# A 32-phase Toeplitz convolution with tree-added LayerNorm statistics, and engine orders from a list scheduler, in a two-layer convolutional decoder trunk

## The chip, the cores and the metric

The kernel runs on the eight NeuronCores of one Trainium2 chip, four on each of two dies. Each core takes one prompt sequence of 2048 positions and 16 decoding sequences of 4 positions, so T = 2112 columns per core, with all weights. The cores do not talk to one another. The time is the device time of the slowest core in microseconds. Some executions of these kernels fall into a slow state, in which the cores of one die show a lower TensorE clock.

TensorE does matrix products into PSUM (eight banks of 512 fp32 columns), VectorE and ScalarE elementwise work, GpSimd (POOL) small copies and the issue of weight loads, SyncE (SP) the issue of the other transfers.

## The reference, cut to what matters

```python
def hybrid_layer(x, ...):                            # twice, then a last RMSNorm
    h = rmsnorm(x, norm_g)
    p = h @ w_in                                     # (T, 7168): a_val, a_gate, z_a, B, C, hb, z_b
    u = a_val * sigmoid(a_gate)
    ca = causal_dwconv(u, width 31)                  # per channel, over positions
    ca = head_layernorm(ca + bias)                   # per token over the 128 channels of a head, 8 heads
    y_a = silu(ca) * silu(z_a)
    y_b = B * causal_dwconv(C * hb, width 3) * silu(z_b)
    return x + concat(y_a, y_b) @ w_out
```

It also returns the last 30 rows of u and the last 2 of C * hb of each sequence. For the decoding sequences 26 of the 30 rows are old ones, copied from input to output by two transfers from memory to memory, one for each layer.

## The kernel before

Activations lie with channels on partitions and columns along the free dimension, in four blocks of 512 and one of 64. A projection of one 128-channel chunk and one block is eight accumulating matmuls. The width-31 convolution is a Toeplitz product: u is written to memory and gathered back so that partitions hold 16 channels x 8 phases (position modulo 8). With 8 phases, 31 taps need five shifts:

```python
PH, CG, NG, NSH = 8, 16, 8, 5
...
for g in range(8):                                   # one head: 8 groups of 16 channels
    bk = pw.next()
    mm_group(bk, banks[bk][:, 0:UROW],               # UROW = 336 columns
             [(toep[:, half, (gg * NSH + s) * 128:...], up_sb[:, g, 64 - 16 * s:UPROW - 16 * s]) for s in range(NSH)], ...)
    P.op("dve", ... tensor_copy(co_sb[...], banks[bk][:, 0:UROW]) ...)
    if lj is not None:                               # LayerNorm statistics of the head before, between the groups
        if 2 <= g < 7: ln_var(g - 2)                 # matmul with 1/128, then Ln
        if g < 5: ln_center(l, lj, g)                # matmul with 0.5*(I - 1/128), then Square
```

Its result goes to memory and back into the channel layout, and the statistics are taken there, with two 512-column matmuls for each block. The Toeplitz blocks are built by VectorE as mask times weights. The order on every engine is the order in which the program writes its operations, interleaved by hand. Weights rotate through seven slots. The state copy of each layer stands late in its layer.

Of the kernel before, what the change touches and what calls it, by code (L numbers as in the profile page):

```python
# [12 lines left out]
D = 1024  # L13
# [14 lines left out]
PH = 8  # L28
CG = 16
NG = 8  # L30
NSH = 5
LANES = 16
UROW = 16 + 64 + 256
UPROW = 64 + UROW
NW = 7
VROW = 272
K_SAME = 3
# [4 lines left out]
class Res:  # L42
    __slots__ = ("name", "w", "r")

    def __init__(self, name):
        self.name = name
        self.w = None
        self.r = []


class Op:
    __slots__ = ("eng", "fn", "deps", "idx", "sig", "cnt", "chan", "name")


class Prog:
    ENGS = ("pe", "act", "dve", "pool", "sp")

    def __init__(self):
        self.ops = {e: [] for e in self.ENGS}
        self.chan_ops = {}  # L60

    def op(self, eng, fn, reads=(), writes=(), chan=None, name=""):
        o = Op()
        o.eng, o.fn, o.chan, o.name = eng, fn, chan, name
        o.sig = False
        o.cnt = 0
        o.idx = len(self.ops[eng])
        deps = set()
        for r in reads:
            if r.w is not None:  # L70
                deps.add(r.w)
        for w in writes:
            if w.w is not None:
                deps.add(w.w)
            for x in w.r:
                deps.add(x)
        deps.discard(o)
        keep = []
        for d in deps:
            if d.chan is None and chan is None and d.eng == eng:  # L80
                if eng == "pe":
                    continue
                if o.idx - d.idx > K_SAME:
                    continue
            keep.append(d)
            d.sig = True
        o.deps = keep
        for r in reads:
            r.r.append(o)
        for w in writes:  # L90
            w.w = o
            w.r = []
        self.ops[eng].append(o)
        if chan is not None:
            self.chan_ops.setdefault(chan, []).append(o)
        return o

    def emit(self, nc, block, sems, chan_sems, final_waits):
        for e in self.ENGS:
            c = 0  # L100
            for o in self.ops[e]:
                if o.chan is None and o.sig:
                    c += 1
                    o.cnt = c
        for ch, lst in self.chan_ops.items():
            c = 0
            for o in lst:
                c += 16
                o.cnt = c
        chan_total = {ch: 16 * len(lst) for ch, lst in self.chan_ops.items()}  # L110

        def run(eng_name):
            def body(e):
                waited = {}
                for o in self.ops[eng_name]:
                    need = {}
                    for d in o.deps:
                        s = chan_sems[d.chan] if d.chan is not None else sems[d.eng]
                        if need.get(s.num, (None, 0))[1] < d.cnt:
                            need[s.num] = (s, d.cnt)  # L120
                    for num, (s, c) in need.items():
                        if waited.get(num, 0) < c:
                            e.wait_ge(s, c)
                            waited[num] = c
                    ins = o.fn(e)
                    if o.chan is not None:
                        ins.then_inc(chan_sems[o.chan], 16)
                    elif o.sig:
                        ins.then_inc(sems[eng_name], 1)
                if eng_name == "sp":  # L130
                    for ch in final_waits:
                        if ch in chan_total:
                            e.wait_ge(chan_sems[ch], chan_total[ch])
            return body

        block.tensor(run("pe"))
        block.scalar(run("act"))
        block.vector(run("dve"))
        block.gpsimd(run("pool"))
        block.sync(run("sp"))  # L140


class Rot:
    def __init__(self, ids):
        self.ids = list(ids)
        self.i = 0

    def next(self):
        v = self.ids[self.i % len(self.ids)]
        self.i += 1  # L150
        return v


def build_nc(wseq=None):


    record = wseq is None
    wused = []
    nc = bass.Bass("TRN2", target_bir_lowering=False)
    P = Prog()  # L160
# [14 lines left out]
    wt_d = din("wt_d", [DEPTH, 8, 128, NG * NSH * PH])  # L175
    cw_b_d = din("cw_b", [128, DEPTH, 8, WB])
    vecs_d = din("vecs", [128, 72])
    hist_a_d = din("hist_a", [DEPTH, 8, 128, NG, 64])
    hist_b_d = din("hist_b", [128, DEPTH, 8, (WB - 1) * NS])
    sa_orig = din("sa_orig", [DEPTH, NS, WA - 1, D])  # L180
    cmat_d = din("cmat", [128, 2, 128])
# [7 lines left out]
    scr_c = dint("scr_c", [DEPTH, 8, 128, PH * UROW], BF16)  # L189
# [3 lines left out]

    x_sb = sb("x_sb", [128, KC * T], F32)
    h_sb = sb("h_sb", [128, KC * T], BF16)
    y_sb = sb("y_sb", [128, 6, T], BF16)
    u_sb = sb("u_sb", [128, 2, PH, UROW], BF16)
    up_sb = sb("up_sb", [128, NG, UPROW], BF16)
    toep = sb("toep", [128, 2, 4 * NSH * 128], BF16)
    co_sb = sb("co_sb", [128, 2, 4, UROW], BF16)  # L200
    cn_sb = sb("cn_sb", [128, PH, UROW], BF16)
    vbuf = sb("vbuf", [128, PH + 2, VROW], BF16)
    wsl = sb("wsl", [128, NW, 1024], BF16)
    wt_sb = sb("wt_sb", [128, 2, NG * NSH * PH], BF16)
    sq = sb("sq", [128, 2, 1024], BF16)
    th_t = sb("th_t", [128, 2, 512], F32)
    sz_t = sb("sz_t", [128, 2, 512], F32)
    rs_t = sb("rs_t", [128, T], F32)
    oat = sb("oat", [128, 3, NOA], F32)
    obt = sb("obt", [128, 8, NOB], F32)  # L210
    histb = sb("histb", [128, DEPTH, 8, (WB - 1) * NS], BF16)
    cmat = sb("cmat_sb", [128, 2, 128], F32)
    mask = sb("mask_sb", [128, 128], BF16)
    cb16 = sb("cb16", [128, 128], BF16)
    ones_s = sb("ones_s", [128, 128], BF16)
    ones_v = sb("ones_v", [128, 128], BF16)
    vecs = sb("vecs_sb", [128, 72], F32)
    cbias = sb("cbias", [128, 16], F32)
    cw_b = sb("cw_b_sb", [128, DEPTH, 8, WB], F32)
    banks = [es.enter_context(nc.psum_tensor(f"psb{i}", [128, 512], F32)) for i in range(8)]  # L220

    R = Res
    x_r = [[R(f"x{k}_{q}") for q in range(NB)] for k in range(KC)]
    h_r = [[R(f"h{k}_{q}") for q in range(NB)] for k in range(KC)]
    y_r = [[R(f"y{s}_{q}") for q in range(NB)] for s in range(6)]
    u_r = [[R(f"u{i}_{q}") for q in range(NB + 1)] for i in range(3)]
    up_r, uph_r = R("up"), R("uph")
    toep_r = [R("toep0"), R("toep1")]
    co_r = [[R(f"co{h}_{g}") for g in range(4)] for h in range(2)]
    cn_r = u_r[2]  # L230
    v_r = [R(f"v{q}") for q in range(NB)]
    vh_r = R("vh")
    w_r = [R(f"w{i}") for i in range(NW)]
    wt_r = [R("wt0"), R("wt1")]
    sq_r = [R("sq0"), R("sq1")]
    th_r = [R("th0"), R("th1")]
    sz_r = [R("sz0"), R("sz1")]
    rs_r = [R(f"rs{q}") for q in range(NB)]
    oat_r = [R("oat0"), R("oat1"), R("oat2")]
    obt_r = [R(f"obt{j}") for j in range(8)]  # L240
    vecs_r, cmat_r, cwb_r, histb_r = R("vecs"), R("cmat"), R("cwb"), R("histb")
    mask_r, cb16_r, ones_r, cbias_r = R("mask"), R("cb16"), R("ones"), R("cbias")
    bank_r = [R(f"bank{i}") for i in range(8)]
    scru_r = [[R(f"scru{l}_{j}") for j in range(8)] for l in range(DEPTH)]
    scrc_r = [[[R(f"scrc{l}_{j}_{h}") for h in range(2)] for j in range(8)] for l in range(DEPTH)]

    def u_view(i):
        return cn_sb if i == 2 else u_sb[:, i]

    pa, pw, pr = Rot([0, 1, 2, 3]), Rot([0, 1, 2]), Rot([4, 5, 6, 7])  # L250
    rot_th, rot_sz, rot_sq = Rot([0, 1]), Rot([0, 1]), Rot([0, 1])
# [9 lines left out]
    def blk(ap, q):  # L261
        if q < 4:
            return ap.rearrange("p (a c) -> p a c", a=2)
        return ap.rearrange("p (a c) -> p a c", a=4)

    def u_blk(ap, q):
        if q < 4:
            return ap[:, 2 * q:2 * q + 2, 80:UROW]
        return ap[:, 0:4, 0:16]

    def v_blk(q, lag):
        if q < 4:
            return vbuf[:, 2 * q + 2 - lag:2 * q + 4 - lag, 0:256]
        return vbuf[:, 2 - lag:6 - lag, 256:272]


    bg = []

    def pop(n=1):
        for _ in range(n):  # L280
            if bg:
                bg.pop(0)()


    wstate = {"loaded": 0, "next": 0}

    def w_prefetch(upto):
        if record:
            return
        while wstate["loaded"] < min(upto, len(wseq)):  # L290
            i = wstate["loaded"]
            s = i % NW
            kind, l, c = wseq[i]
            src = w_in_r[l, c] if kind == "in" else w_out_r[l, c]
            P.op("pool", (lambda e, s=s, src=src: e.dma_start(out=wsl[:, s, :], in_=src)),  # L295
                 reads=([x_r[7][0]] if i == 2 else []), writes=[w_r[s]], chan=f"w{s}", name=f"wload{i}")
            wstate["loaded"] += 1

    def w_get(*keys):
# [585 lines left out]
```

## Time and profile before

| | before |
|---|---|
| median of fast and slow runs, by session | 1334.5 to 1338.9 us |
| span of the profiled run | 1334.8 us |
| TensorE busy | 1215.7 us |
| VectorE, ScalarE, GpSimd busy | 715.7, 495.2, 135.4 us |
| TensorE work at issue cost (worked out in the prediction) | 1169 us |

The issue cost of a matmul is the time from its start to the next one's start in a dense run; the work is the sum of these. Three numbers make the time: this work, what TensorE's busy time has over it (matmuls at half clock, and drains: the end of the last matmul before a gap), and TensorE's idle time. The prediction works out all three and shows the lines. In a view, L318 is line 318 of that run's kernel.py; a line of waits ends with the total in us, how often, and the longest.

### The profile page before, as it was taken

What the parts mean: (1) busy time and instruction counts of PE and PEld (TensorE: products, weight loads), DVE (VectorE), ACT (ScalarE), POOL (GpSimd) and SP (SyncE); (2) the same over time, 40 slices, a digit from 0 to 9 for tenths busy, and PEclk for the clock granted to TensorE, in tenths of its full rate; (3) what the DMA queues carried; (4) which work ended last, traced back from release to release, by engine and by line L of the source; (5) the groups of instructions that cost most, each with busy time, mean ns of one, the idle gap of its engine ahead of it and who ended that gap; (6) DMA issues with size and microseconds to landing.
All of it is one profiled execution on the core that took longest, in us unless ns stands there. A gap on an engine that the chain in (4) does not pass through costs nothing.

```text
span 1334.8 us, 20305 instructions; the slowest of 8 cores (1324.8 to 1334.8 us)
## 1 busy us (share of the span) xinstructions
PE 1215.7 (91%) x6682; PEld 573.9 (43%) x6682; DVE 715.7 (54%) x1297; ACT 495.2 (37%) x805; POOL 135.4 (10%) x264
## 2 busy tenths in 40 slices
PE   3778999989998999999989699999999899999986
PEld 1233444444443444444444344444444344444442
DVE  4443445467564484445652345546746548444555
ACT  4430555551554402222331055555055440222232
POOL 1011111100101001000010211110010100100000
PEclk9898999999999999999989899999999999999988
DMA  9317655523436113212020674542343610322033
GB/s 266 67 52 136 161 128 128 108 41 73 100 64 124 24 17 59 37 32 37 1 42 18 153 176 116 117 116 64 62 102 54 136 25 16 56 41 32 13 130 131
DMA packets 88101, 108.61 MB, mean 81 GB/s; under 512 B 24960, under 2 KB 60288, under 8 KB 87552
## 3 DMA queue, kind: packets, MB, share of 16 engines
q0 software_dynamic: 39824, 41.30, 21.0%
q1 hardware_dynamic: 47744, 65.82, 15.6%
q8 instruction: 57, 0.93, 0.3%
q14 instruction: 44, 0.36, 0.1%
q10 hardware_dynamic: 432, 0.19, 0.1%
HBM read 116.85 MB, written 35.14 MB: 114 GB/s over the span
## 4 chain that ended last, share of the span: by engine, by line
PE 86%; DMA 5%; DVE 3%; issue 3%; ACT 2%; DVEq 0%; SPq 0%; POOL 0%; ACTq 0%; POOLq 0%
PE psb L318 85%; DMA wsl<-w_in_r 3%; PE psb L382 1%; DMA x_sb<-x_d 1%; DMA cn_sb<-scr_c 1%; ACT rs_t L530 1%; DVE x_sb L628 1%; ACT sq L368 0%; DVE h_sb L400 0%; DVE sz_t L614 0%; DVE toep L474 0%; ACT L392 0%; ACT rs_t L392 0%; DMA scr_c<-co_sb 0%; DVE co_sb L491 0%
## 5 line engine op out<-in xcount | busy, mean ns | idle before, releaser
L318 PE MATMUL psb<-h_sb,wsl 128*128 128x512 bf16 (+1 forms) x4480 | 819.9, 346 | 36.0 <-DMA wsl<-w_in_r 24.4
L318 PEld LDWEIGHTS psb<-h_sb,wsl 128*128 128x128 bf16 x4480 | 381.8, 99 | 474.7 <-issue 61.0
L628 DVE TENSOR_TENSOR x_sb<-x_sb,psb 128x512 f32<-128x512 f32 (+1 forms) x240 | 138.7, 592 | 62.9 <-PE psb L318 58.9
L318 PE MATMUL psb<-y_sb,wsl 128*128 128x512 bf16 (+1 forms) x800 | 160.1, 343 | 8.2 <-DVE x_sb L628 6.7
L318 PE MATMUL psb<-up_sb,toep 128*128 128x336 bf16 x640 | 110.9, 308 | 20.8 <-ACT rs_t L530 10.6
L579 DVE TENSOR_TENSOR vbuf<-psb,th_t 128x512 bf16<-128x512 f32 (+1 forms) x80 | 47.5, 597 | 134.5 <-PE psb L318 121.6
L605 DVE SCALAR_TENSOR_TENSOR rs_t<-vbuf,cw_b_sb,rs_t 128x512 f32<-128x512 bf16 (+1 forms) x160 | 104.9, 655 | 18.1 <-POOL vbuf L588 9.4
L430 DVE SCALAR_TENSOR_TENSOR u_sb<-th_t,psb 128x512 bf16<-128x512 f32 (+1 forms) x70 | 41.5, 593 | 132.7 <-PE psb L318 91.1
L575 ACT ACTIVATE th_t<-psb 128x512 f32<-128x512 f32 (+1 forms) x80 | 41.3, 516 | 183.3 <-PE psb L318 183.3
L318 PEld LDWEIGHTS psb<-y_sb,wsl 128*128 128x128 bf16 x800 | 69.1, 98 | 87.0 <-issue 14.0
L491 DVE CAST co_sb<-psb 128x336 bf16<-128x336 f32 x128 | 64.5, 507 | 71.8 <-PE psb L318 71.4
L427 ACT ACTIVATE th_t<-psb 128x512 f32<-128x512 f32 (+1 forms) x80 | 41.3, 517 | 142.8 <-PE psb L318 140.5
L610 ACT ACTIVATE sz_t<-psb 128x512 f32<-128x512 f32 (+1 forms) x80 | 41.8, 522 | 139.4 <-PE psb L318 139.4
L561 ACT ACTIVATE sz_t<-psb 128x512 f32<-128x512 f32 (+1 forms) x80 | 40.0, 521 | 133.2 <-PE psb L318 132.4
L368 ACT ACTIVATE sq<-x_sb 128x1024 bf16<-128x1024 f32 (+1 forms) x60 | 53.3, 903 | 97.2 <-DVE x_sb L628 77.8
L563 DVE TENSOR_TENSOR y_sb<-rs_t,sz_t 128x512 bf16<-128x512 f32 (+1 forms) x80 | 46.5, 598 | 79.7 <-ACT sz_t L561 79.7
L295 POOL DMA_DIRECT2D wsl<-w_in_r x112 | 60.2, 544 | 258.3 <-PE psb L318 241.3
L318 PEld LDWEIGHTS psb<-up_sb,toep 128*128 128x128 bf16 x640 | 57.5, 97 | 65.0 <-issue 38.8
L551 ACT ACTIVATE rs_t<-rs_t,vecs_sb 128x512 f32<-128x512 f32 (+1 forms) x80 | 57.5, 734 | 42.3 <-DVE rs_t L548 42.0
L318 PE MATMUL psb<-y_sb,toep 128*128 128x512 bf16 (+1 forms) x320 | 71.4, 348 | 0.0
L382 PE MATMUL psb<-sq,ones_s 128*128 128x512 bf16 (+1 forms) x120 | 34.0, 380 | 33.6 <-ACT sq L368 23.5
L548 DVE SCALAR_TENSOR_TENSOR rs_t<-psb,cbias,rs_t 128x512 f32<-128x512 f32 (+1 forms) x80 | 49.7, 651 | 27.0 <-ACT rs_t L507 27.0
(59 smaller groups left out, 749.6 us busy)
## 6 DMA issues: line engine op xcount, KB each, us to landing
wsl<-w_in_r POOLq DMA_DIRECT2D x112, 256.0 KB, 6.3
up_sb<-scr_u SPq DMA_DIRECT2D x16, 672.0 KB, 8.9
scr_c<-co_sb SPq DMA_DIRECT2D x32, 336.0 KB, 2.9
cn_sb<-scr_c SPq DMA_DIRECT2D x16, 672.0 KB, 7.9
scr_u<-u_sb SPq DMA_DIRECT2D x14, 672.0 KB, 3.7
x_sb<-x_d SPq DMA_DIRECT2D x3, 2048.0 KB, 19.4
wsl<-w_out_r POOLq DMA_DIRECT2D x24, 256.0 KB, 4.4
oa_copy<-sa_orig SPq DMA_DIRECT2D x2, 1664.0 KB, 15.1
```

Of the source, the lines that this page charges most:

```text
L295: P.op("pool", (lambda e, s=s, src=src: e.dma_start(out=wsl[:, s, :], in_=src)), reads=([x_r[7][0]] if i == 2 else []), writes=[w_r[s]], c ...
L318: ins = e.matmul(out, lhsT=l_, rhs=r_, start=(i == 0), stop=(i == len(pairs) - 1))
L368: P.op("act", (lambda e: e.activation(out=sq[:, s, 0:2 * n], in_=x_sb[:, KC * c0 + 2 * kp * n:KC * c0 + (2 * kp + 2) * n], func=AF.Square) ...
L382: ins = e.matmul(banks[bk][:, 0:n], lhsT=ones_s[:], rhs=sq[:, s, i * n:(i + 1) * n], start=(kp == 0 and i == 0), stop=(kp == 3 and i == 1))
L491: P.op("dve", (lambda e, bk=bk, half=half, gg=gg: e.tensor_copy(co_sb[:, half, gg, :], banks[bk][:, 0:UROW])), reads=[bank_r[bk]], writes= ...
L548: P.op("dve", (lambda e: e.scalar_tensor_tensor(out=r_ap, in0=banks[bk][:, 0:n], scalar=cbc, in1=r_ap, op0=ALU.add, op1=ALU.mult)), reads= ...
L551: P.op("act", (lambda e: e.activation(out=r_ap, in_=r_ap, func=AF.Silu, scale=gcol, bias=bcol)), reads=[rs_r[q], vecs_r], writes=[rs_r[q]] ...
L563: P.op("dve", (lambda e, r_ap=r_ap, iz=iz, n=n, q=q: e.tensor_tensor(out=y_ap(slot, q), in0=r_ap, in1=sz_t[:, iz, 0:n], op=ALU.mult)), rea ...
L579: P.op("dve", (lambda e, bh=bh, it=it, n=n, q=q: e.tensor_tensor(out=v_blk(q, 0), in0=blk(banks[bh][:, 0:n], q), in1=blk(th_t[:, it, 0:n], ...
L605: P.op("dve", (lambda e, a_ap=a_ap, q=q, lag=lag: e.scalar_tensor_tensor(out=a_ap, in0=v_blk(q, lag), scalar=cw_b[:, l, j, 2 - lag:3 - lag ...
L610: P.op("act", (lambda e, bz=bz, iz=iz, n=n: e.activation(out=sz_t[:, iz, 0:n], in_=banks[bz][:, 0:n], func=AF.Silu)), reads=[bank_r[bz]], ...
L628: P.op("dve", (lambda e: e.tensor_tensor(out=xv(m, q), in0=xv(m, q), in1=banks[bk][:, 0:n], op=ALU.add)), reads=[bank_r[bk], x_r[m][q]], w ...
```

## The change

Four things at once.

1. **32 phases x 4 channels.** Partitions hold 4 channels x 32 phases. 31 taps need two shifts, and each group has 80 to 96 columns. One head is 32 groups of two matmuls; four groups share a PSUM bank.
2. **LayerNorm in that layout.** All channels of one token lie in 4 partitions x 32 blocks, so VectorE adds the 32 blocks down to 4 in bf16 and a matmul with a 0/1 pattern (over 128) adds those and the four partitions. Subtract, square, add again, scale; then the result goes to memory and back.
3. **A list scheduler.** The program records operations with estimated durations; a simulation gives each engine's order, and the slots of weights, PSUM banks and temporaries.
4. Smaller things: the Toeplitz blocks are copied at four offsets into zeroed tiles, the history is scaled on GpSimd, eight weight slots, the first stage also holds group B's first two projections.

```diff
-PH = 8
-CG = 16
-NG = 8
-NSH = 5
+PH = 32
+CG = 4
+NG = 32
...
+                for gi in range(4):
+                    ...
+                    e.matmul(o, lhsT=toep[:, tp.slot, (m + 1) * 128:(m + 2) * 128],
+                             rhs=up_sb[:, g, :].rearrange("p (i c) -> p i c", i=2)[:, :, 0:48], start=True, stop=False)
+                    ins = e.matmul(o[:, 16:96], lhsT=toep[:, tp.slot, m * 128:(m + 1) * 128], rhs=up_sb[:, g, 48:128],
+                                   start=False, stop=True)
...
+        def tree(src, dst):
+            dve(... big[:, dst.slot, 0:16, :] = big[:, src.slot, 0:16, :] + big[:, src.slot, 16:32, :] ...)
+            for h in (8, 4):
+                dve(... big[:, dst.slot, 0:h, :] += big[:, dst.slot, h:2 * h, :] ...)
+            mm("stat", b, CROW, [(same, big[:, dst.slot, i, :]) for i in range(4)], ...)
...
+    def run(self):            # the scheduler: each free engine takes the ready operation with the lowest key
...
+              4.3, [scru_r[l][j]], [up_r], "up", name=f"up{j}")          # the model's duration of the gather
...
-        P.op("sp", (lambda e, l=l: e.dma_start(out=oa_copy[l], in_=sa_orig[l, :, DS:WA - 1, :])), chan="copy")
+        spdma((lambda e, l=l: e.dma_start(out=oa_copy[l], in_=sa_orig[l, :, DS:WA - 1, :])), 8.0, (), (), "copy", name="copy")
```

## The prediction

> **What bounds the kernel now.** I read the views in this order: busy time per engine and the 40 slices, the chain that ended last, the groups by line and form, the windows by stage, and last the timeline around one convolution. The page first:
>
> ```profile
> PE 1215.7 (91%) x6682; PEld 573.9 (43%) x6682; DVE 715.7 (54%) x1297; ACT 495.2 (37%) x805; POOL 135.4 (10%) x264
> ...
> PEclk9898999999999999999989899999999999999988
> ...
> PE 86%; DMA 5%; DVE 3%; issue 3%; ACT 2%; DVEq 0%; SPq 0%; POOL 0%; ACTq 0%; POOLq 0%
> ```
>
> TensorE is busy 91% of the 1334.8 us span and is 86% of the chain; VectorE is at 54%. So the time is TensorE's work, plus what TensorE idles, plus what it loses at a lower clock. The groups by form say what that work is, and which of it the change touches:
>
> ```profile
> L318 PE MATMUL psb<-h_sb,wsl 128*128 128x512 bf16 x3584 | 799.4, 384 | 33.8 <-DMA wsl<-w_in_r 24.4 <-DVE h_sb L400 5.2 <-DVE co_sb L491 2.6
> ...
> L318 PE MATMUL psb<-up_sb,toep 128*128 128x336 bf16 x640 | 110.9, 308 | 20.8 <-ACT rs_t L530 10.6 <-ACT sz_t L561 4.3 <-DVE sz_t L614 4.3
> ...
> L318 PE MATMUL psb<-sq,ones_v 128*128 128x512 bf16 x64 | 25.4, 397 | 7.3 <-ACT sq L522 4.1 <-DVE sz_t L614 2.4 <-DVE u_sb L617 0.8
> L318 PE MATMUL psb<-cn_sb,cb 128*128 128x512 bf16 x64 | 24.7, 392 | 1.0 <-DMA cn_sb<-scr_c 1.0
> ```
>
> The projections dominate and do not change. The Toeplitz convolution (640 matmuls of 336 columns) and the two LayerNorm matmuls per block (centring and variance, 64 of 512 columns each) do. The means are latencies of overlapping instructions; the cost of one is its spacing. The timeline (start, duration) gives it:
>
> ```profile
> 334.52 0.88 PE L318 MATMUL psb<-up_sb,toep 128*128 128x336 bf16 x5
> 335.24 0.38 PE L318 MATMUL psb<-cn_sb,cb 128*128 128x512 bf16 x1
> 335.45 0.88 PE L318 MATMUL psb<-up_sb,toep 128*128 128x336 bf16 x5
> ```
>
> Five convolution matmuls take 335.24 - 334.52 = 0.72 us, 143 ns each; one of 512 columns takes about 0.216 us. For short ones I need the 64-column matmuls of a sample block, in two nested windows (columns: busy time and count of PE, weight loads, VectorE, ...):
>
> ```profile
> 357.20:357.30 0.10, 0.10 (x6) 0.10 (x5) 0.00 (x0) 0.00 (x0) 0.00 (x0) 1.00 0.00 0
> 357.20:357.50 0.30, 0.30 (x13) 0.30 (x12) 0.07 (x1) 0.00 (x0) 0.00 (x0) 1.00 0.00 0
> ```
>
> The longer one holds seven more matmuls and seven more weight loads in 0.2 us more: 29 ns for a 64-column matmul with its own weights. So a short matmul is not held up by its weight load.
>
> Where TensorE idles, by stage (the last columns are clock, DMA share, GB/s):
>
> ```profile
> 0.00:42.00 42.00, 16.82 (x51) 5.01 (x52) 16.57 (x20) 16.12 (x18) 6.45 (x15) 0.96 0.95 255
> 42.00:127.00 85.00, 65.80 (x354) 30.52 (x353) 35.31 (x81) 26.57 (x40) 8.90 (x15) 0.90 0.34 72
> 127.00:690.00 563.00, 535.31 (x2966) 254.53 (x2967) 320.31 (x566) 220.39 (x363) 58.71 (x116) 0.98 0.34 69
> 690.00:745.00 55.00, 44.36 (x244) 20.57 (x243) 13.12 (x39) 9.71 (x17) 7.20 (x12) 0.93 0.37 72
> 745.00:1257.00 512.00, 491.89 (x2745) 235.04 (x2744) 286.53 (x516) 198.99 (x337) 54.16 (x106) 0.99 0.37 79
> 1257.00:1334.80 77.80, 61.57 (x329) 28.18 (x327) 43.89 (x77) 23.43 (x30) 0.00 (x0) 0.90 0.31 112
> ```
>
> Idle is 25 + 19 + 28 + 11 + 20 + 16 = 119 us. Over a third of it lies before 127 us. One clear case, from the timeline (start, duration, instruction, idle before it and what ended it):
>
> ```profile
> 106.51 14.62 PE L318 MATMUL psb<-h_sb,wsl 128*128 128x512 bf16 x72 [9.64 <-DMA wsl<-w_in_r]
> ```
>
> The first stage of a layer holds six of the seven weight slots to its end, so six loads start together when it is over and TensorE waits 9.6 us. This recurs in layer 1 (10.3 us at 744.6).
>
> **What the Trainium skill says.** (1) "TensorE: Matmul & The Clock Gate", Back-to-back issue gap: N/2.4 + 2.5 ns for an isolated warm matmul, but about 81 ns at N=128 in a stream of weight load and matmul. The trace agrees with the formula at 336 and 512 columns (143, 216 ns) and at 64 (29 ns), and not with a weight-load bound. (2) Same page, Part 1: after an idle window of some 3.4 us the array falls to half clock. The trace agrees: clock 0.90 and 0.93 where the idle is, 0.98 and 0.99 elsewhere. (3) "VectorE: DVE Perf Modes", the perf-mode tier table: bf16 tensor_tensor at 2x, bf16 tensor_copy at 4x. The trace: a 2560-element bf16 product takes 1486 ns (0.15 us + 2560/960/2), a 512-element bf16 scale 291 ns (0.16 + 512/960/4). (4) "SBUF — State Buffer", SBUF: two separate sides: a VectorE operation with two SBUF inputs, and a GpSimd one that reads SBUF, exclude each other. The trace agrees: a pool copy of 0.58 us took 1.65 us when it met a Toeplitz product at 733 us.
>
> **The change, part by part.** TensorE. Issue cost before: 512-column matmuls 3584 + 640 + 256 + 128 = 4608 x 0.2158 = 994.5; their 64-column ones 1152 x 0.029 = 33.6; convolution 640 x 0.1425 = 91.2; LayerNorm 128 x 0.2158 + 32 x 0.029 = 28.5; RMSNorm 96 x 0.2158 + 24 x 0.029 = 21.4. Sum 1169 us. After: with 32 phases every lag fits in two shifts, so a head takes 32 groups x (96 + 80 columns). By the formula that is 32 x (42.5 + 35.8) = 2.5 us, over 16 heads 40 us. LayerNorm needs two times four matmuls of 80 columns, 8 x 0.036 = 0.29 us a head, 4.6 us in all. Saved: 91.2 - 40.1 + 28.5 - 4.6 = 75 us, leaving 1094 us. All of it is on TensorE, which is the path.
>
> VectorE. Removed: evacuation casts 64.5, Toeplitz products 47.5, the normalising products 46.4 + 4.5, history 4.7, memsets some 7; 175 us. Added per head: 8 evacuations with bias of 320 elements, 0.16 + 0.33 = 0.49 us, 3.9; 16 copies of 512 at 4x, 0.29 us, 4.7; two add trees (1280, 640, 320 at 2x: 0.82 + 0.49 + 0.32), 3.3; subtract and scale over 2560, 2 x 1.49 = 3.0. Sum 14.9, over 16 heads 238 us. VectorE goes to about 780 us. That is under TensorE's by 300 us, so it should lie beside it.
>
> ScalarE. Removed per head: five squares, five Ln, two Exp, and two table loads, in all (43.8 + 5.5 + 38.5 + 3.6 + 17.6 + 16.8 + 41.0)/16 = 10.4 us. Added: one square of 2560, about 0.2 + 2560/1200 = 2.3, three small ones 0.75, and two table loads 2.6. It falls by about 75 us, to 420. More to the point, the chain variance matmul, table load, Ln no longer holds PSUM banks between convolution groups: those waits (12.0 us on rs_t L530, some 8 on the squares and z gates around it) should go.
>
> DMA. The gather of u now moves runs of 192 bytes, the scatter of the convolution 160 bytes, 4096 packets each, not 1024 of 672. In the packet records a 672-byte packet takes 33 ns and a 192-byte one 15 ns, so 256 packets per engine take 3.8 us, not 2.1. With the next head's work in between that should be hidden. Weights do not change.
>
> Scheduler. The first stage needs six of eight slots, so two weights for the next part can be loaded ahead: the 9.6 and 10.3 us waits should go. In the start the second block's RMSNorm no longer stands ahead of the first projection (28.3 us now); I expect it near 23 to 25, as more weight loads compete with the first x block. The rest of the start is set by 8.6 MB of x at 255 GB/s, some 34 us, and stays.
>
> Idle after, my estimates by stage: start 44 to 26 us, layer boundary 11 to 3, the two middles 48 to 24 (fixed orders from a cost model leave some), end 16 to 15 (the last block's norm and store are as before). Sum 68, against 119. The 46 us by which busy time exceeds issue cost now (1215.7 - 1169) are half clock and drains after gaps; with little more than half the gaps I take 25. So 1094 + 68 + 25 = 1187 us of span, and the runs' median lies 7 us over the span of the profile. I choose **1188 us**, a little under that sum, because list-scheduled order with rotating slots could leave less idle in the middles.
>
> **Rivals.** (a) Weight loads bind the short matmuls: at the skill's 81 ns, 1024 x 81 = 83 us for the convolution instead of 40, and 43 us of the saving are lost: 1230 us. The 29 ns spacing speaks against it. (b) VectorE becomes the bound locally: its 15 us per head come in a burst with operations of 1.5 us, and behind them PSUM banks wait. Two convolution banks against 0.49 us evacuations and 0.31 us of matmuls make a pure convolution VectorE-bound. Average load 780 of 1188, 66%, and five projection banks speak against it; if it failed I would see 30 to 50 us more idle: 1230. (c) The frozen order meets other DMA or pool durations than its model (shared port, short runs) and TensorE waits on weights or on the gathered u: 1220 to 1300. Against it: slack of nearly a head (68 us of TensorE work). (d) The schedule is near perfect: idle only at both ends, 1094 + 45 + 15 + 7 = 1161.
>
> **Range and chances.** (d) and part of (b) or (c) bound the range: 1150 to 1228. Even (a) alone stays 8% below 1341.6; to lose the 2% needs over 120 us of new waits. Faster 0.95, same 0.03, slower 0.02.
>
> **What would show it.** Right: convolution matmuls spaced about 39 ns, their busy near 45 to 60 us and not 111; LayerNorm statistics under 10 us; VectorE 760 to 800 and ScalarE about 420 us busy; no wait on a weight load over 3 us at a layer's start; clock over 0.98 in the middle. Wrong: convolution spacing of 60 ns or more (a); large waits of TensorE on VectorE tiles (b); on weight or gather transfers (c).

## The result and the profile after

The changed kernel takes **1225.1 us** (median of 4; three fast runs from 1222.2 to 1227.4) against 1338.9 us. The ratio is 0.916 (0.912 to 0.919). All ratios here are the mean time of one kernel's fast runs over that of the other's fast runs of the same rounds, so they are not quite the ratio of the medians. The time lies in the predicted range, near its upper end: 37 us above the point.

The page of the changed kernel:

```profile
PE 1122.4 (92%) x7032; PEld 544.0 (45%) x7032; DVE 763.5 (63%) x1547; ACT 436.0 (36%) x681; POOL 191.4 (16%) x336
...
PEclk9669988999999999999999999999999999999998
...
PE 77%; DMA 15%; DVE 3%; issue 1%; ACT 1%; another core or an unknown queue 1%; POOL 0%; DVEq 0%; SPq 0%; ACTq 0%; POOLq 0%
```

TensorE's busy time fell by 93 us. The chain that ended last now holds 15% of DMA, where it held 5%. The clock is 0.9 or more of full speed but in the second and third of the 40 slices (0.6), the sixth and seventh, and the last (0.8).

The groups by line and form (columns as before): the convolution's two matmuls and the statistics' one.

```profile
L643 PE MATMUL psb<-up_sb,toep 128*128 128x96 bf16 x512 | 50.8, 211 | 20.6 <-DMA up_sb<-scr_u 20.5
L645 PE MATMUL psb<-up_sb,toep 128*128 128x80 bf16 x512 | 50.4, 203 | 0.0
...
L529 PE MATMUL psb<-big,same 128*128 128x80 bf16 x128 | 9.8, 200 | 2.0 <-DVE big L665 1.8
```

The two busy times overlap and must not be added. In a dense run the next matmul starts 43 ns after one of 96 columns and 35 ns after one of 80 (medians in the trace), 39 ns on average. 20.5 us of waits on the gather of u stand before them.

The windows by stage (the start, the first convolution, the rest of layer 0, the boundary, the rest of layer 1, the end):

```profile
0.00:140.00 140.00, 85.33 (x382) 34.21 (x383) 46.60 (x98) 48.98 (x67) 23.86 (x41) 0.85 0.56 122
140.00:190.00 50.00, 36.59 (x248) 18.59 (x247) 24.30 (x58) 9.05 (x14) 9.32 (x16) 0.88 0.69 128
190.00:660.00 470.00, 465.84 (x2977) 228.99 (x2976) 325.87 (x649) 182.12 (x286) 76.74 (x133) 1.00 0.49 85
660.00:760.00 100.00, 92.91 (x591) 45.69 (x589) 55.29 (x124) 26.23 (x45) 17.86 (x33) 0.97 0.51 94
760.00:1150.00 390.00, 381.93 (x2508) 188.72 (x2505) 267.60 (x544) 145.81 (x239) 63.66 (x114) 1.00 0.53 93
1150.00:1221.30 71.30, 59.79 (x338) 27.75 (x335) 43.81 (x78) 23.84 (x31) 0.00 (x0) 0.93 0.31 122
```

Idle is 54.7 + 13.4 + 4.2 + 7.1 + 8.1 + 11.5 = 99.0 us. The two long middles, 860 us together, hold only 12 us of it: there TensorE is full. The first 190 us hold 68 us, more than the first 127 us of the kernel before (44 us).

What TensorE waited for at the start, in the timeline of the changed kernel (start, duration, instruction, idle before it):

```profile
7.46 47.38 SPq L907 DMA_DIRECT2D oa_copy<-sa_orig  x2
...
54.61 3.57 PE L529 MATMUL psb<-h_sb,wsl 128*128 128x512 bf16 x8 [8.22 <-DMA wsl<-w_in_r]
...
70.73 3.57 PE L529 MATMUL psb<-h_sb,wsl 128*128 128x512 bf16 x8 [8.76 <-DMA wsl<-w_in_r]
```

Two waits for a weight are over 8 us long. The first line is not seen in the kernel before: both state copies are issued on the SP queue between 7.5 and 54.8 us, layer 1's too. They read nothing that the kernel makes, so the scheduler found them ready at time zero. Before, they were issued at 393.5 and 1034.3 us. The copies' packets run from 40.5 to 70.2 us. The trace's records of single packets say what happens to the weights in three stretches of that time (packets that start in the stretch; their durations, summed and divided by the 16 DMA engines):

```
stretch      state copy, 53248-byte packets   weights, 2048-byte packets
40 to 44 us       16 packets, 4.6 us                78 packets, 1.2 us
44 to 48 us       12 packets, 3.6 us                15 packets, 0.4 us
60 to 64 us       13 packets, 4.1 us                 1 packet
```

A 53248-byte packet takes 4.75 us (median), a weight packet 0.17 us. All 64 of the copies' packets together take 18.7 us of each of the 16 engines, on average. From 52 to 60 us, mostly between the two copies, 255 weight packets start. In the third stretch the records don't tell how many weight packets were waiting. The longest time to landing of a weight went from 24.7 us before to 61.5 us.

### The profile page after: what moved, and what is told of

Read it like the earlier page. It is cut to its first block, busy times and chain, and to the rows that moved or that the text cites. A ratio compares the mean times of both kernels' runs of the same rounds, so it can differ in the third digit from the quotient of the medians.

```text
span 1221.3 us, 20545 instructions; the slowest of 8 cores (1206.9 to 1221.3 us)
## 1 busy us (share of the span) xinstructions
PE 1122.4 (92%) x7032; PEld 544.0 (45%) x7032; DVE 763.5 (63%) x1547; ACT 436.0 (36%) x681; POOL 191.4 (16%) x336
## 4 chain that ended last, share of the span: by engine, by line
PE 77%; DMA 15%; DVE 3%; issue 1%; ACT 1%; another core or an unknown queue 1%; POOL 0%; DVEq 0%; SPq 0%; ACTq 0%; POOLq 0%
PE psb L529 74%; DMA up_sb<-scr_u 5%; DMA wsl<-w_in_r 4%; DMA scr_c<-big 2%; PE psb L643 2%; DMA scr_u<-u_sb 1%; PE psb L645 1%; DMA big<-scr_c 1%; DVE x_sb L567 1%; DMA wt_sb<-wt_d 1%; DVE h_sb L567 1%; DVE big L682 0%; DVE toep L621 0%; DVE x_sb L777 0%
## 5 line engine op out<-in xcount | busy, mean ns | idle before, releaser
L529 PE MATMUL psb<-h_sb,wsl 128*128 128x512 bf16 (+1 forms) x4480 | 835.3, 346 | 40.5 <-DMA wsl<-w_in_r 28.3
L584 DVE SCALAR_TENSOR_TENSOR u_sb<-tmp,psb 128x512 bf16<-128x512 f32 (+1 forms) x80 | 47.3, 592 | 122.3 <-PE psb L529 112.2
L759 DVE SCALAR_TENSOR_TENSOR tmp<-vbuf,cw_b_sb,tmp 128x512 f32<-128x512 bf16 (+1 forms) x160 | 103.9, 655 | 26.4 <-POOL vbuf L741 11.9
L582 ACT ACTIVATE tmp<-psb 128x512 f32<-128x512 f32 (+1 forms) x80 | 41.8, 523 | 196.8 <-PE psb L529 189.8
L621 DVE COPY toep<-wt_sb 32x512 bf16<-32x512 bf16 x256 | 78.2, 307 | 37.4 <-DMA wt_sb<-wt_d 20.8
L729 DVE TENSOR_TENSOR vbuf<-psb,tmp 128x512 bf16<-128x512 f32 (+1 forms) x80 | 47.3, 594 | 59.9 <-PE psb L529 59.4
L550 ACT ACTIVATE tmp<-x_sb 128x1024 bf16<-128x1024 f32 (+1 forms) x60 | 52.9, 904 | 87.9 <-DVE x_sb L777 76.7
L764 ACT ACTIVATE tmp<-psb 128x512 f32<-128x512 f32 (+1 forms) x80 | 41.7, 523 | 112.3 <-PE psb L529 101.1
L650 DVE TENSOR_TENSOR big<-psb,cbt_sb 128x320 bf16<-128x320 f32 x128 | 62.3, 486 | 26.2 <-PE psb L645 23.1
L756 ACT ACTIVATE tmp<-vbuf,cw_b_sb 128x512 f32<-128x512 bf16 (+1 forms) x80 | 51.6, 644 | 65.0 <-DVE vbuf L729 49.0
L718 ACT ACTIVATE tmp<-psb 128x512 f32<-128x512 f32 (+1 forms) x80 | 40.6, 523 | 86.1 <-PE psb L529 75.3
L643 PE MATMUL psb<-up_sb,toep 128*128 128x96 bf16 x512 | 50.8, 211 | 20.6 <-DMA up_sb<-scr_u 20.5
L727 ACT ACTIVATE tmp<-psb 128x512 f32<-128x512 f32 (+1 forms) x80 | 40.5, 516 | 71.7 <-PE psb L529 69.6
L713 ACT ACTIVATE tmp<-big,vecs_sb 128x512 f32<-128x512 bf16 (+1 forms) x80 | 55.4, 732 | 17.5 <-DMA big<-scr_c 15.1
```

What stands on the lines that cost most here:

```text
L529: ins = e.matmul(bank(v, n), lhsT=l_(), rhs=r_(), start=(first and i == 0), stop=(last and i == len(pairs) - 1))
L550: act((lambda e, s=s, kp=kp: e.activation(out=tmph[:, s.slot, 0:2 * n], in_=x_sb[:, KC * c0 + 2 * kp * n:KC * c0 + (2 * kp + 2) * n], func ...
L584: dve((lambda e: e.scalar_tensor_tensor(out=u_blk(ub, q), in0=b3(tm(th, n), q), scalar=1.0, in1=b3(bank(bv, n), q), op0=ALU.add, op1=ALU.m ...
L621: dve((lambda e, p=p, c=c: e.tensor_copy(toep[p, tp.slot, :].rearrange("p (m x) -> p m x", x=128)[:, :, 32 * c:32 * c + 32], wt_sb[p, w.sl ...
L643: e.matmul(o, lhsT=toep[:, tp.slot, (m + 1) * 128:(m + 2) * 128], rhs=up_sb[:, g, :].rearrange("p (i c) -> p i c", i=2)[:, :, 0:48], start ...
L650: dve((lambda e, b=b, v=v, bias=bias: e.tensor_tensor(out=big[:, co.slot, 4 * b:4 * b + 4, :], in0=banks[v.slot][:, 0:384].rearrange("p (g ...
```

## The experiments

All twelve gave right results, and each was timed in three rounds beside the kernel before. Differences in microseconds below are worked out from ratios: (ratio of one / ratio of the other - 1) x the time of the other.

### The state copies

Theory A is that the copies, issued at once, starve the weight loads; B is that the start is bound by its bytes anyway. Two runs from opposite sides: hold the copies back in the changed kernel, and bring them forward in the kernel before.

```diff
- ... 8.0, (), (), "copy", name="copy")
+ ... 8.0, (), (), "copy", after=[S.ops[-1]], name="copy")      # after the layer's last gate product
```

> The changed kernel with one edit: the two state copies (1.66 MB read and 1.66 MB written each) may start only after the last gate product of their layer; in the changed kernel nothing held them back and both were issued at 7.5 us. Theory A (the copies starve the weight loads at the start: their 53248-byte packets take 4.75 us each, 64 of them are 18.7 us on all 16 engines, and the weights take turns with them packet by packet): the waits of TensorE on weight loads (28.3 us in all) fall to under 14 us, and the time falls by 15 to 28 us, from 1225 to 1197 to 1210. Theory B (the start is bound by the sum of x, eight weight blocks, history and Toeplitz weights, whatever the copies do): at most 6 us less, 1219 or more.

Measured: 1197.6 us, ratio 0.897 (0.894 to 0.900), that is 2.1% or 25 us less than the changed kernel. TensorE's half-clock time before 100 us fell with the waits, from 41.0 to 20.5 us.

```diff
 # kernel before, in setup() after the x loads; the copy at its old place is removed
+for l in range(DEPTH):
+    P.op("sp", (lambda e, l=l: e.dma_start(out=oa_copy[l], in_=sa_orig[l, :, DS:WA - 1, :])), chan="copy")
```

> The kernel before with one edit: both state copies are issued right after the x loads, where the changed kernel's schedule put them. Theory A: it loses 12 to 28 us at the start, 1339 to 1351 to 1367. Theory B: within 5 us of 1339.

Measured: 1353.5 us, ratio 1.014 (1.011 to 1.016), 18 us more: clear of the noise. The waits on weights, in the order changed kernel, copy_late, before_copy_early, kernel before:

```profile
PE psb L529 <- DMA wsl<-w_in_r: 28.3, 7, 8.8
```

```profile
PE psb L529 <- DMA wsl<-w_in_r: 11.8, 4, 6.2
```

```profile
PE psb L318 <- DMA wsl<-w_in_r: 41.5, 5, 17.0
```

```profile
PE psb L318 <- DMA wsl<-w_in_r: 24.4, 3, 10.3
```

Theory A holds on both sides, and B falls: the same transfers cost 18 us in a kernel without any scheduler. The copies move the same bytes in all four kernels; only their moment differs. What these runs show is that the moment of the copies costs the time. That it costs it through the length of their packets, and not just through their bytes, is read from the packet records; no run issues the copies early in short packets.

### The gather of u in the cost model

```diff
-              4.3, [scru_r[l][j]], [up_r], "up", name=f"up{j}")
+              8.0, [scru_r[l][j]], [up_r], "up", name=f"up{j}")
```

> The changed kernel with one number changed: the schedule's cost model takes 8.0 us, not 4.3, for the gather of u (measured median to landing 8.3 us, longest 18.7). No instruction is added or removed, only orders move. Theory C (the 20.5 us of waits on the gather come from the model's too short duration): waits on the gather fall below 8 us and the time falls by 8 to 15 us, to 1210 to 1217. Theory D (the long gathers are the ones that take turns with a burst of weight loads after a layer's first stage, and another fixed order meets the same burst): the wait changes place, the time stays within 5 us of 1225. The model itself puts this schedule 7 us longer than the other (1166 against 1159).

Measured: 1208.1 us, ratio 0.904 (0.902 to 0.906), 1.3% or 16 us less. The waits on the gather, changed kernel and then this run:

```profile
PE psb L643 <- DMA up_sb<-scr_u: 20.5, 4, 7.2
```

```profile
PE psb L643 <- DMA up_sb<-scr_u: 2.2, 1, 2.2
```

Theory C holds, with a gain just over its 8 to 15 us. No instruction was added or taken away; the convolution's place in TensorE's order moved. A part of what D expected came too: the waits on weights grew from 28.3 to 33.6 us. The gather is not slow because of its short runs alone: its 192-byte packets take 15 ns, so 256 per engine take 3.8 us, near what the model had. But it runs at a layer's start beside a burst of weight loads. In the packet records of the changed kernel from 145 to 150 us the engines served 226 packets of 192 bytes and 279 of 2048, nearly one each in turn, though one lasts twelve times as long as the other. The 16 gathers took 5.6 to 18.7 us, median 8.3. It is of note that the model rated the better schedule 7 us worse (1166 against 1159 us).

### Long packets of x

```diff
-  spdma(... x_sb[:, KC * c0:KC * (c0 + n)] ..., f"x{q}")
+  for i in range(4):
+      lo, m = KC * c0 + 2 * i * n, 2 * n
+      spdma(... x_sb[:, lo:lo + m] ..., f"x{q}{i}")
```

> As copy_late, and each x block from the second on is loaded in four transfers, so that its packets have 4096 and not 16384 bytes (about 165 and not 690 ns each). Theory A2 (packets of the two queues alternate, so the longer packets of x starve the weights too): another 5 to 15 us less than copy_late, and the first stage's waits on weights nearly gone. Theory B2 (the bytes bind): within 3 us of copy_late, with the wait moved from the weights to x.

Measured: 1184.8 us, ratio 0.886 (0.883 to 0.890), 14 us less than copy_late. Theory A2's size holds, but the waits on weights were not nearly gone, as it expected: 9.7 us after 11.8, one of them 7.9. What fell was the sum of TensorE's waits on weights, on squares of the next x block (19.8 to 15.8 us) and on h, the normalised block (6.6 to 4.0). Its half-clock time before 100 us is 6.8 us, against 20.5 in copy_late. So the gain is shown, and A2's account of it only in part.

> The kernel before with x from the second block on loaded in four transfers (packets of 4096, not 16384 bytes). If the starving of weight loads behind long x packets belongs to any kernel that loads both at once, it gains too: 4 to 10 us (it waits 4.4 us for a weight at 38 us, and 9.6 us at 98 us, which the x loads do not cause and which stays). If it comes only from the changed kernel's eight weight loads at once: within 3 us of 1336.

Measured, for the same edit in the kernel before: 1326.8 us, ratio 0.994 (0.993 to 0.996), 8 us less, in the expected 4 to 10. The cost of long packets at the start is not one of the change's own.

### The three together

> The changed kernel with the three edits together: state copies late, x blocks after the first in four transfers, gather 8.0 us in the cost model. If the three costs are separate, the gains add: 1225 - 27 (copies) - 13 (x) - 17 (gather) = 1168 us. If late copies and short x packets already shorten the weight waits that the other order avoids, part is counted twice: 1172 to 1182. Over 1182: the orders work against each other.

Measured: **1174.1 us**, ratio 0.879 (0.877 to 0.881): 49 us less than the changed kernel, where the single gains add to 25 + 14 + 16 = 55. It lies in the range that was given for a part counted twice. Its page:

```profile
PE 1114.1 (95%) x7032; PEld 542.0 (46%) x7032; DVE 763.6 (65%) x1547; ACT 435.4 (37%) x681; POOL 191.3 (16%) x336
```

Idle is 1173.0 - 1114.1 = 58.9 us, and busy over issue cost 1114.1 - 1094.1 = 20 us. It is the version that beats both kernels.

> all_three with 10.0, not 8.0 us for the gather in the cost model; the longest measured are 18 to 20 us, at the start of a layer. If longer is still safer: 1166 to 1172 (one wait of 4.5 us on a gather is left at 124 us). If what is left are waits that only move: 1171 to 1178.

Measured: 1172.4 us, ratio 0.878 (0.877 to 0.880), which overlaps all_three's. A longer estimate brings no gain that these runs can tell: the 4.5 us wait on the gather went, and waits on weights grew from 13.0 to 17.2 us.

### What TensorE's saved work is worth

```diff
-                for gi in range(4):
+                for gi in (0, 1, 2, 3, 0, 1, 2, 3):      # c_pe in the cost model doubled as well
```

> The changed kernel with every group of eight convolution matmuls issued twice into the same bank (the second starts the sum anew, so results stay right), the cost model told of it. It adds 16 x 32 x (42.5 + 35.8) ns = 40 us of TensorE issue. Theory P (the time is TensorE's issue cost plus fixed losses, so the 51 us that the new layout took out of the convolution are worth 51 us): plus 36 to 44 us, 1261 to 1269. Theory W (the convolution sits where TensorE waits for VectorE or DMA anyway): plus 10 to 25 us only. Theory L (short matmuls cost more than their columns, bound by their weight loads): the added matmuls show more than 50 us and a spacing over 45 ns.

Measured: 1249.6 us, ratio 0.938 (0.933 to 0.943), 30 us more than the changed kernel, between P (36 to 44) and W (10 to 25); with the intervals of both ratios it is 22 to 38 us, so this run does not decide. L falls: the spacings are 43 and 35 ns with twice as many, as before. I repeated it on all_three, where a layer's start was thought to hold almost no waits.

> conv_twice cost 25 to 30 us where 40 were added, and in its trace layer 1 had 11 us less idle at its start than the changed kernel. Here the same doubling is put on all_three (1174 us), whose layer starts hold almost no such waits to be swallowed. Theory P (the doubled matmuls cost their issue time, the missing 12 us were waits that the other order happened to avoid): plus 34 to 42 us, 1208 to 1216. Theory W (a part of the convolution is always hidden in waits): plus 20 to 30 us again, 1194 to 1204.

Measured: 1202.9 us, ratio 0.902 (0.900 to 0.903), 30 us more than all_three (27 to 33 with both intervals): less than P said, and at the upper end of W's range. The trace tells where the rest is. From the first convolution matmul of head 4 to that of head 7, in the dense part of a layer, all_three takes 172.9 to 173.5 us on all eight cores and in both layers, all_conv_twice 180.1 to 182.0 us. The medians, 173.0 and 180.1, give (180.1 - 173.0) / 3 = 2.4 us a head, where 2.5 were added: nearly full price. From head 0 to head 4, where 10 us were added, the medians of the eight cores differ by layer: in layer 0 164.7 us became 165.6 (single cores 161.4 to 168.3), in layer 1 162.9 became 172.8 (172.6 to 173.6). So nearly all of the missing 40 - 30 us was swallowed in one place, the first four heads of layer 0. Three of all_three's waits:

```profile
PE psb L643 <- DMA up_sb<-scr_u: 4.5, 1, 4.5
...
PE psb L643 <- DVE toep L621: 3.5, 1, 3.5
PE psb L529 <- DMA big<-scr_c: 2.6, 2, 2.1
```

All three lines, 10.6 us, are missing in all_conv_twice. The first two lie between 110 and 300 us, at layer 0's first convolutions; the third comes after 300 us. The expectation's premise was wrong there: layer 0 still held waits to be swallowed. Where TensorE waits for a transfer or another engine, more of its work fits beside the wait at little cost; where it is full, work costs what it takes. So P is right for the dense part and for layer 1, and W for the first heads of layer 0.

### VectorE's new work

> The changed kernel with each of the 256 copies that build the Toeplitz blocks done twice (same data), the cost model told of it: about 78 us more on VectorE, 763 to 841 us busy. Theory P (VectorE's new work lies beside TensorE's): plus 0 to 12 us; the cost model's own schedule grows by 9. Theory V (VectorE is locally the bound around a convolution): plus 25 us or more.

The edit runs each of the 256 copies twice (`for c in (0, 1, 2, 3, 0, 1, 2, 3)`). Measured: 1229.2 us, ratio 0.920 (0.918 to 0.922), 0.5% or 6 us more, with VectorE at 828.9 us busy and not 763.5 (78 us more were expected, 65 came). The interval overlaps the changed kernel's, so the 6 us are not clear of the noise. Theory P holds and V falls: 65 us more on VectorE cost 6 or nothing.

```diff
-            (three VectorE additions of the tree)
-            mm("stat", b, CROW, [(same, big[:, dst.slot, i, :]) for i in range(4)], ...)
+            mm("stat", b, CROW, [(same, big[:, src.slot, i, :]) for i in range(NG)], ...)
```

> all_three without the bf16 add trees: the 32 blocks of a head are summed over channels by 32 matmuls of 80 columns in one group, for the mean and again for the variance, not by three VectorE additions and four matmuls. TensorE gets 16 x 2 x 28 x 35.8 ns = 32 us more, VectorE 16 x 3.3 = 53 us less. Theory P (TensorE is the bound and VectorE has slack): 1174 + 26 to 34 = 1200 to 1208. Theory V (the trees' latency on VectorE holds up the evacuations): less than 15 us more, or a gain.

Measured: 1198.1 us, ratio 0.897 (0.896 to 0.899), 24 us more than all_three, a little under P's 26. Heads 4 to 7 take 178.9 to 180.9 us: at the median of 179.5, 2.2 us a head, where 2.0 were added. In layer 0 the stretch from head 0 to head 4 again takes 164.7 us, as in all_three, with 8 us of work added. The add tree earns its place: it moves 32 us of estimated work from the full engine to one that has room, and saves 24.

### The order

> The changed kernel with the list scheduler made to keep TensorE, ScalarE and VectorE in the order in which the program writes their operations; layout, instructions, slots and the two DMA queues' freedom are as in the changed kernel. It tells how much of the result hangs on the interleaving and how much on the layout alone. Theory S (the layout's long dependent chain, conv, tree, square, tree, scale, must be spread between projections, or TensorE waits at every step): far slower than the kernel before, 1450 to 1600 (the cost model says 1545). Theory T (layout carries the gain, order is worth what the idle time was worth): under 1330.

The edit makes the scheduler take an operation on TensorE, ScalarE or VectorE only if it is the next that the program wrote there. Measured: 1638.0 us, ratio 1.226 (1.223 to 1.229), slower than the kernel before by 23%, and beyond the 1450 to 1600 that theory S gave. Theory S holds in kind. Two lines of its waits:

```profile
PE psb L649 <- DVE toep L627: 169.2, 60, 4.4
PE psb L535 <- DVE big L671: 150.9, 32, 6.8
```

TensorE waits 60 times for the Toeplitz blocks, which are built 64 times, and for each of the 32 trees, and the mean clock falls to 0.845. This is no fair contest with a hand-made order, since the program is not written to be run in its order. It shows that the new layout in this order is no gain. How much the layout would bring in a good hand-made order, and the scheduler with the old layout, no run shows.

## Why the prediction was right, and where it was off

**TensorE's work: right.** The matmuls of the traces times the issue costs give 1094.1 us, as predicted. Short matmuls are not bound by their weights: the spacings are 43 and 35 ns, 39 on average, as predicted. Rival (a) falls.

**VectorE and ScalarE: right.** 763.5 and 436.0 us busy, against about 780 and 420. Both lie beside TensorE; rival (b) falls by toep_copies_twice and all_no_tree.

**The waits behind the variance and Ln: right; the sum of the middles: partly luck.** No wait of TensorE behind Ln is left in the trace. The two middles were given 24 us of idle. The stretches that I call middles hold 12, but the first convolution, which the prediction's middle took in and mine does not, holds another 13.4. So the sum came out at 25.7 because a wait on the gather took the place of what was saved.

**The weight wait at layer 1's start: right.** There is no wait over 3 us for a weight after the first 100 us of the changed kernel; before, 10.3 us.

**The start: wrong, and this is the step that failed.** The prediction said "start 44 to 26 us" and "the rest of the start is set by 8.6 MB of x at 255 GB/s". It measures 54.7 us before 140 us: 29 of the 31 us by which the idle time exceeds the estimate. The first projection came at 22.0 us, even before the 23 to 25 expected, so the step fails after it. The step took for granted that the start would hold the same transfers as before. It overlooked that an operation without inputs is ready at once for a list scheduler: 25 us of the changed kernel's time are the two state copies, whose cost is shown from both sides (18 us in the kernel before). Another 14 us go when x comes in short packets; how they are lost is shown only in part.

**The gather: mis-sized.** "256 packets per engine take 3.8 us ... with the next head's work in between that should be hidden." The packet time was right (15 ns), the landing was 8.3 us in the median and up to 18.7, and at a layer's start there is no head's work in between: 13.4 us of idle from 140 to 190 us, and 16 us of time. Rival (c) and the list of what would show it had named waits on weights and on the gather.

**Busy over issue cost: right,** 1122.4 - 1094.1 = 28 us, 25 predicted.

So 113.5 us between the profiled spans are 75 us of work, 119 - 99 = 20 us of idle, and 46 - 28 = 18 us of half clock and drains. This split is worked out from the traces and not from runs that change one part alone. With the three causes of the miss taken away the kernel stands at 1174 us, 14 under the point of 1188, and its idle of 59 us is near the 68 of the sum. The range held because a part of rival (c) was in it, not because the start was understood: the median lies 3 us from its end. The prediction's own sum with the runs' 7 us was 1194 us; the choice of 1188, for less idle in the middles, made the miss 6 us larger.

What stays open: how much of x_split's 14 us is the turns of packets and how much the earlier first quarters of each x block, and whether the early copies cost their 25 us through packet length or through bytes alone; no run separates them.

## What to carry to other kernels

When a scheduler orders operations by readiness, look for those that depend on nothing, most of all large transfers, and hold them back to where their queue is idle. Estimate a transfer's landing from what shares the engines at that moment, not from its own packets: in these records two queues with work took turns by packet (226 packets of 192 bytes against 279 of 2048), so the one with the longer packets got most of the time. Work moved off a full engine is worth its issue cost where that engine is full (2.4 of 2.5 us a head here), and less where it waits for transfers anyway (1 of 10 us in layer 0's first heads).

## What the Trainium skill lacked or had wrong

- "TensorE: Matmul & The Clock Gate", Back-to-back issue gap: about 81 ns per matmul at N=128 in a stream of weight load and matmul. Here the next matmul starts 43 ns after one of 96 columns, 35 ns after one of 80 and 29 ns after one of 64, each with its own weights; no run has 128 columns.
- The same page, Part 1, speaks of idle windows of some 3.4 us. In copy_late an idle of 2.33 us before 558.8 us was enough for 3.4 us at half clock from 559.5 us on, though TensorE was busy for 1.07 us between 556.0 and 559.4 us.
- "DMA: Bandwidth & Descriptors", Queues, rings and completion order: it has round-robin at packet granularity, and the records agree where both queues had work (226 and 279 packets from 145 to 150 us). It lacks what follows when packets differ in length: from 44 to 48 us 12 packets of 53248 bytes (4.75 us each) in one queue left room for 15 of 2048 bytes (0.17 us) in the other, and a weight load took up to 61.5 us to land.
- The same page, Specifications, says that transfers under 512 bytes are read, modified and written. The 160-byte packets of the scatter to memory took 14 ns (median) and 192-byte ones of the gather 15 ns, against 22 ns for 384 bytes and 33 ns for 672 in the kernel before: dearer per byte, but with no step at 512 bytes to be seen in these records.
